# Moving the small tiles ahead of the large ones: a layout change in a hybrid gMLP and pooling layer

## The chip, the cores and the metric

The kernel runs on one core of one Trainium2 chip. The metric is the device time of one execution in microseconds; times given for a kernel are the median of several executions. One execution was also taken by the hardware profiler, and everything said about single instructions, waits and transfers comes from that one.

## The reference

One layer works on 4096 prompt frames and on 32 sample frames, with 1024 channels each. Cut to what matters here:

```python
h = rmsnorm(x, norm_g)
proj = jnp.einsum('btd,de->bte', h, w_in)                 # 1024 -> 5120
u, v, z_a, xb, z_b = jnp.split(proj, [...], axis=-1)      # five of 1024
v_n = layernorm(v, ln_v_g, ln_v_b)
a = u * chunk_mlp(v_n, w_spatial, b_spatial) * jax.nn.silu(z_a)   # 128x128 mixing of positions per head
b = pool_mix(x_ext, pos0, w_pool, pool_scale) * jax.nn.silu(z_b)  # windows 2/4/8/16, 256x256 map per group
y = x + jnp.einsum('bte,ed->btd', jnp.concatenate([a, b], axis=-1), w_out)   # 2048 -> 1024
return y, x_ext[:, -POOL_STATE:], v_n                     # y goes through a last rmsnorm
```

All inputs and outputs are float32. The outputs are the normalised y of prompt and sample, the last 15 pooling rows of both, and the v rows of the sample.

## The kernel before

**Products.** Each large product is cut into 2 x 2 blocks and made from seven block products in place of eight (the additions of the blocks before and after are on VectorE and ScalarE). Each operand is split into a high and a low part in the type float32r, and a block product is the sum of high x high, high x low and low x high. So a block product of one kind is 12 matmuls: four steps of 128 channels (k), three matmuls each. In the shared helper these are lines 175, 176 and 177; in the output product they are lines 698, 699 and 700. The moving operand is 512 columns wide, except in the last block of tokens, where 16 sample frames are added to each half and a product runs over two groups of 264 columns.

**Stages.** First the projection v is made for all tokens (0 to about 404 us of the span; moving operand: the weights of v, stationary operand: the split tokens). Then four blocks of 1024 tokens each go through eight gate sets (u and z of branch A, with the spatial mixing at line 913) and eight pool sets (the pooling map folded into the input weights, and z of branch B); here the moving operand is the tokens and the stationary one the split weights. The last two stages are the two halves of the output product (from about 1736 us on); the moving operand is the weights, the stationary one the split results.

**Tiles.** The moving operands lie in seven slots of 16896 bytes in each partition (pool slots, tile slot), one per block product, reloaded at each change of stage. In a block of tokens that is not the last, a slot holds for each part h and each channel step k four pieces of 128 columns, which stand 2048 bytes apart; one matmul reads all four. In the output stages and for v it reads 512 columns in one piece. In the last block of tokens the piece of part h and step k starts (4h + k) x 2112 bytes into the slot, and the second group of 264 columns 1056 bytes further. Loaded weights and results come into tiles raw (4096 bytes), are split into tiles wop (4096 bytes: high parts of four steps, then low parts), and sums go to tiles sum (2048 bytes). The v stage has tiles xt, op, h and et of the same kind in the same space. Results are gathered in tiles t (2176 bytes) and y (4096 bytes). Small tiles of 16 to 96 bytes (pool smallp) hold sums of squares, means and inverse roots; each name has its own ring of two.

**Where a tile lies.** Pools are laid one behind the other in each partition, in the order in which they are opened, and each tile is rounded up to a multiple of 32 bytes. Ahead of everything stand 16512 bytes that the kernel does not name; then the pool const (512 + 32 + 32 + 32 + 512 bytes), then the slots, then smallp, then the pools of the stages. So the slots start at byte 17632, and behind the 118272 bytes of slots and the 896 of smallp the stage pools start at 136800. The v tiles are laid from the other end and do not follow this order.

**Order.** The order of instructions on each engine is that of the code, with the preparation of operands (additions and splits) running five block products ahead of the matmuls that use them and the loads seven ahead. Loads go through the queue of SyncE, stores of results through that of GpSimd.

The lines that the change touches, besides the two pools: psc (the pooling scales), the small tile of OutPair.finish at line 718, and the two small tiles of OutSample at lines 754 and 775.

Of the kernel before, what the change touches and what calls it, by code (L numbers as in the profile page):

```python
# [8 lines left out]
F32 = mybir.dt.float32  # L9
# [6 lines left out]
P = 128  # L16
D = 1024
KT = D // P
SEQ = 4096
DEC = 32  # L20
# [16 lines left out]
def stream_step(ctx: ExitStack, tc, x_prompt, x_sample, state_pool, norm_g, w_in, ln_v_g, ln_v_b,  # L37
# [14 lines left out]
    w_out_v = w_out[0].rearrange("(k p) e -> k p e", p=P)  # L52

    const = ctx.enter_context(tc.tile_pool(name="const", bufs=1))
    slots = ctx.enter_context(tc.tile_pool(name="slots", bufs=NQ))
    smallp = ctx.enter_context(tc.tile_pool(name="smallp", bufs=2))
    dram = ctx.enter_context(tc.tile_pool(name="dram", bufs=1, space=bass.MemoryType.DRAM))

    abT = dram.tile([16, P, TOT], F32, name="abT")
# [11 lines left out]
    make_identity(nc, ident)  # L71
    lvg = const.tile([P, HEADS], F32, name="lvg")
    lvb = const.tile([P, HEADS], F32, name="lvb")
    psc = const.tile([P, KT], F32, name="psc")
    ppast = const.tile([P, KT, HALO], F32, name="ppast")

    def small(tag, n, rows=P):
        return smallp.tile([P, 8], F32, tag=tag, name=tag)[:rows, :n]
# [4 lines left out]
    def rsqrt(a, n, rows=P):  # L83

        y, t = small("rs_y", n, rows), small("rs_t", n, rows)
        nc.vector.tensor_single_scalar(t.bitcast(I32), a.bitcast(I32), 1, ALU.logical_shift_right)
        nc.vector.tensor_scalar(y.bitcast(I32), t.bitcast(I32), -1.0, float(0x5F3759DF), ALU.mult, ALU.add)
        for _ in range(3):
            nc.vector.tensor_tensor(t, y, y, ALU.mult)
            nc.vector.scalar_tensor_tensor(t, t, -0.5, a, ALU.mult, ALU.mult)  # L90
            nc.vector.scalar_tensor_tensor(y, t, 1.5, y, ALU.add, ALU.mult)
        return y
# [547 lines left out]
    class OutPair:  # L640
# [50 lines left out]
        def multiply(self, q):  # L691
            own = {0: 0, 1: 1, 2: 0, 3: 3, 4: 0, 5: 5, 6: 3}[q]
            if own == q:
                self.acc[own] = acc_tile()
            x, w = self.ops[q], w_slots[self.z, q]
            a, fresh = self.acc[own], own == q
            for k in range(4):
                mm(a, x[:, 0, k, :], w[:, k, 0], start=fresh and k == 0, stop=False, skip_group_check=True)  # L698
                mm(a, x[:, 0, k, :], w[:, k, 1], start=False, stop=False, skip_group_check=True)  # L699
                mm(a, x[:, 1, k, :], w[:, k, 0], start=False, stop=k == 3, skip_group_check=True)  # L700
            for n, h, bank in {0: [(0, 0, 0)], 1: [(0, 0, 1)], 2: [(1, 0, 0)], 3: [(1, 1, 3)], 4: [(0, 1, 0), (1, 1, 0)],
                               5: [(0, 1, 5)], 6: [(1, 0, 3)]}[q]:
                y = self.y[n][:, h * 512:(h + 1) * 512]
                nc.vector.tensor_tensor(y, self.acc[bank], y, ALU.add)  # L704
            if self.z and q in (1, 4, 5, 6):
                n, h = {1: (0, 0), 4: (1, 1), 5: (0, 1), 6: (1, 0)}[q]
                junk = sum_p.tile([P, 2 * 512], BF16, tag="sum", name="junk")[:, :512]
                nc.scalar.activation(junk, self.y[n][:, h * 512:(h + 1) * 512], AF.Square,
                                     accum_out=self.ss[:, n, h:h + 1])

        def finish(self, last=None):
            t0 = 2 * self.i * P
            if self.z == 0:
                for n in range(2):
                    nc.gpsimd.dma_start(part[t0 + n * P:t0 + (n + 1) * P, :], self.y[n])
                return
            tiles = (0, 1) if last is None else (last,)
            a = small("ssa", 2)
            ss, a = self.ss[:, tiles[0]:tiles[-1] + 1], a[:, :len(tiles)]
            nc.vector.tensor_tensor(a, ss[:, :, 0], ss[:, :, 1], ALU.add)  # L720
            nc.vector.tensor_scalar(a, a, 1.0 / D, EPS, ALU.mult, ALU.add)
            r = rsqrt(a, len(tiles))
            for n in tiles:
                y = self.y[n]
                for z, c in enumerate((slice(0, 512), slice(512, D)) if last is not None else (slice(0, D),)):
                    nc.vector.scalar_tensor_tensor(y[:, c], y[:, c], r[:, n - tiles[0]:n - tiles[0] + 1], f_bc[:, c],
                                                   ALU.mult, ALU.mult)
                    queue = nc.gpsimd if last is None else (nc.sync, nc.scalar)[z]
                    queue.dma_start(yp[t0 + n * P:t0 + (n + 1) * P, c], y[:, c])

    class OutSample:
# [19 lines left out]
        def multiply(self):  # L751
            b, w = self.both, w_slots
            if self.z:
                ss = small("sss", 2, DEC)
            for n, terms in enumerate(([(k, 0, k) for k in range(4)] + [(4 + k, 1, k) for k in range(4)],
                                       [(8 + k, 5, k) for k in range(4)] + [(12 + k, 3, k) for k in range(4)])):
                acc = more_tile()
                for i, (st, q, k) in enumerate(terms):
                    wq = w[self.z, q]
                    if i < 7:  # L760
                        mm(acc[:2 * DEC], b[:, st, :], wq[:, k, 0], start=i == 0, stop=False)  # L761
                    mm(acc[:DEC], b[:, st, :DEC], wq[:, k, 1], start=False, stop=False)  # L762
                mm(acc[:2 * DEC], b[:, st, :], wq[:, k, 0], start=False, stop=True)
                low = sum_p.tile([P, 512], F32, tag="sum", name="low")[:DEC]
                y = self.y[:, n * 512:(n + 1) * 512]
                nc.scalar.copy(low, acc[DEC:2 * DEC])
                nc.vector.tensor_tensor(y, low, y, ALU.add)
                nc.vector.tensor_tensor(y, acc[:DEC], y, ALU.add)
                if self.z:
                    junk = sum_p.tile([P, 2 * 512], BF16, tag="sum", name="junk")[:DEC, :512]  # L770
                    nc.scalar.activation(junk, y, AF.Square, accum_out=ss[:, n:n + 1])
            if self.z == 0:
                nc.gpsimd.dma_start(part[SEQ:], self.y)
                return
            a = small("ssb", 1, DEC)
            nc.vector.tensor_tensor(a, ss[:, :1], ss[:, 1:], ALU.add)
            nc.vector.tensor_scalar(a, a, 1.0 / D, EPS, ALU.mult, ALU.add)
            r = rsqrt(a, 1, DEC)
            nc.vector.scalar_tensor_tensor(self.y, self.y, r, f_bc[:DEC], ALU.mult, ALU.mult)
            nc.gpsimd.dma_start(ys, self.y)  # L780
# [303 lines left out]
    with ExitStack() as ph:  # L1084
# [7 lines left out]
        def more_tile():  # L1092
            return ps_more.tile([P, 512], F32, tag="more", name="more")
# [110 lines left out]
```

## Time and profile before

| | |
|---|---|
| median of 3 runs | 2397.96 us (2397.54 to 2403.63) |
| the profiled execution | 2398.71 us, span 2396.9 us |
| mean granted TensorE clock | 0.998 |
| TensorE matmul busy | 2375.3 us (99% of the span), 11924 instructions |
| weight loads busy | 1986.0 us (83%) |
| VectorE busy | 1795.2 us (75%) |
| ScalarE busy | 893.3 us (37%) |
| GpSimd busy | 201.3 us (8%) |
| moved by DMA | 445.69 MB, mean 186 GB/s |

How to read it: matmuls are pipelined, so the duration that a row shows for one matmul (about 0.4 us) is longer than the time from its start to the start of the next one. The pace of TensorE is read from starts and counts, not from durations; but where one matmul of a steady row takes longer than another, its duration grows too.

### The profile page before, as it was taken

To read this page: it belongs to the slowest core of one execution; us is meant where nothing else is said; L and a number is where in the kernel's file an instruction comes from. 1 tells how busy PE (TensorE), PEld (TensorE's weight loads), DVE (VectorE), ACT (ScalarE), POOL (GpSimd) and SP (SyncE) were. 2 spreads that over 40 slices of the span, in tenths; PEclk is the share of its full clock that TensorE was granted. 3 is DMA by queue.
4 is the path that set the end of the run, shared out by engine and by line. 5 is a ranking of instruction groups with operands and counts; after the bars stand their busy time and mean duration, and the time that the engine had idled before them with its cause. 6 is when DMAs were issued, how large, how long until landed. Compare 5 with 4: busy or idle time off the path is not lost.

```text
span 2396.9 us, 32564 instructions
## 1 busy us (share of the span) xinstructions
PE 2375.3 (99%) x11924; PEld 1986.0 (83%) x11924; DVE 1795.2 (75%) x3322; ACT 893.3 (37%) x1599; POOL 201.3 (8%) x394
## 2 busy tenths in 40 slices
PE   8999999999999999999999999999999999999998
PEld 6878887788888888888888899999977778888876
DVE  6877777766777667877668776668767777598887
ACT  6545444333433333333334333333322332233332
POOL 1010000100011000110001110102200000000000
PEclk9999999999999999999999999999999999999999
DMA  8878977432448334474334472334687777855432
GB/s 298 315 236 278 272 248 236 133 104 87 144 141 289 97 97 132 132 281 132 106 106 141 166 263 90 99 99 151 225 319 255 259 257 233 306 180 164 158 127 82
DMA packets 325289, 445.69 MB, mean 186 GB/s; under 512 B 19340, under 2 KB 248460, under 8 KB 322440
## 3 DMA queue, kind: packets, MB, share of 16 engines
q1 hardware_dynamic: 273384, 354.79, 45.2%
q0 software_dynamic: 22288, 73.48, 8.4%
q10 hardware_dynamic: 29456, 15.34, 2.4%
q8 instruction: 94, 1.54, 0.3%
q14 instruction: 67, 0.55, 0.1%
HBM read 273.88 MB, written 169.66 MB: 185 GB/s over the span
## 4 chain that ended last, share of the span: by engine, by line
PE 95%; DMA 3%; DVE 2%; ACT 0%; issue 0%; SPq 0%; DVEq 0%; ACTq 0%
PE acc L175 22%; PE acc L177 22%; PE acc L176 22%; PE acc L698 8%; PE acc L699 8%; PE acc L700 8%; PE sp L913 2%; PE tr L456 1%; DMA vt<-in_w_in_dram 1%; DMA wops<-raw 1%; DMA slot<-wops 1%; DMA op<-in_w_in_dram 0%; PE more L762 0%; DVE y L704 0%; PE more L761 0%
## 5 line engine op out<-in xcount | busy, mean ns | idle before, releaser
L175 PE MATMUL acc<-slot,wop 128*128 128x512 f32 (+1 forms) x2240 | 792.0, 354 | 2.1 <-ACT t L151 1.2
L177 PE MATMUL acc<-slot,wop 128*128 128x512 f32 (+1 forms) x2240 | 784.7, 351 | 0.0
L176 PE MATMUL acc<-slot,wop 128*128 128x512 f32 (+1 forms) x2240 | 784.5, 350 | 0.0
L175 PEld LDWEIGHTS acc<-slot,wop 128*128 128x128 f32 x2240 | 422.2, 188 | 61.2 <-ACT t L151 1.7
L177 PEld LDWEIGHTS acc<-slot,wop 128*128 128x128 f32 x2240 | 421.4, 188 | 60.1 <-DVE wop L81 0.3
L176 PEld LDWEIGHTS acc<-slot,wop 128*128 128x128 f32 x2240 | 422.1, 188 | 57.9 <-issue 0.2
L81 DVE TENSOR_TENSOR wop<-raw,wop 128x512 fp32r<-128x512 f32 x510 | 353.0, 695 | 154.7 <-ACT wop L106 137.7
L106 ACT CAST wop<-raw 128x512 fp32r<-128x512 f32 x340 | 210.5, 621 | 401.5 <-PE acc L177 321.0
L698 PE MATMUL acc<-slot,wop 128*128 128x512 f32 x896 | 353.8, 395 | 1.8 <-DMA slot<-wops 1.1
L699 PE MATMUL acc<-slot,wop 128*128 128x512 f32 x896 | 353.6, 395 | 0.0
L700 PE MATMUL acc<-slot,wop 128*128 128x512 f32 x896 | 353.2, 395 | 0.0
L149 DVE TENSOR_TENSOR t<-acc,t 128x512 f32<-128x512 f32 (+1 forms) x320 | 186.6, 584 | 129.8 <-ACT t L158 72.4
L704 DVE TENSOR_TENSOR y<-acc,y 128x512 f32<-128x512 f32 x256 | 173.4, 687 | 96.1 <-PE acc L700 94.7
L698 PEld LDWEIGHTS acc<-slot,wop 128*128 128x128 f32 x896 | 168.7, 188 | 43.8 <-ACT wop L660 2.4
L700 PEld LDWEIGHTS acc<-slot,wop 128*128 128x128 f32 x896 | 168.7, 188 | 39.6
L699 PEld LDWEIGHTS acc<-slot,wop 128*128 128x128 f32 x896 | 168.7, 188 | 39.2
L175 PE MATMUL acc<-slot,op 128*128 128x512 f32 x448 | 182.0, 407 | 0.3 <-ACT vt L151 0.2
L176 PE MATMUL acc<-slot,op 128*128 128x512 f32 x448 | 176.8, 395 | 0.0
L177 PE MATMUL acc<-slot,op 128*128 128x512 f32 x448 | 176.7, 396 | 0.0
L660 ACT CAST wop<-raw 128x512 fp32r<-128x512 f32 x160 | 97.9, 620 | 185.1 <-PE acc L700 172.3
L81 DVE TENSOR_TENSOR wop<-sum,wop 128x512 fp32r<-128x512 f32 x200 | 137.0, 685 | 30.0 <-ACT wop L106 24.6
L932 POOL DMA_DIRECT2D abT<-t x128 | 69.2, 541 | 874.6 <-DVE t L944 634.8
(213 smaller groups left out, 2489.3 us busy)
## 6 DMA issues: line engine op xcount, KB each, us to landing
raw<-in_w_in_dram SPq DMA_DIRECT2D x102, 512.0 KB, 4.3
xops<-op SPq DMA_DIRECT2D x72, 512.0 KB, 6.3
abT<-t POOLq DMA_DIRECT2D x128, 256.0 KB, 3.5
raw<-abT SPq DMA_DIRECT2D x64, 512.0 KB, 4.9
slot<-xops SPq DMA_DIRECT2D x30, 1024.0 KB, 10.6
slot<-wops SPq DMA_DIRECT2D x14, 2048.0 KB, 8.5
xt<-in_x_prompt_dram SPq DMA_DIRECT2D x32, 512.0 KB, 5.3
raw<-v_all SPq DMA_DIRECT2D x32, 512.0 KB, 3.4
```

The source lines that it names most:

```text
L81: return nc.vector.tensor_tensor(out, src, hi.bitcast(F32), ALU.subtract)
L106: pair = nc.scalar.copy(hi, src), lo_part(lo, src, hi)
L149: add = lambda o, x, y: nc.vector.tensor_tensor(o, x, y, ALU.add)
L175: mm(acc, sh, mh, start=fresh and k == 0, stop=False, skip_group_check=True)
L176: mm(acc, sh, ml, start=False, stop=False, skip_group_check=True)
L177: mm(acc, sl, mh, start=False, stop=k == 3, skip_group_check=True)
L660: nc.scalar.copy(t[:, 0], src)
L698: mm(a, x[:, 0, k, :], w[:, k, 0], start=fresh and k == 0, stop=False, skip_group_check=True)
L699: mm(a, x[:, 0, k, :], w[:, k, 1], start=False, stop=False, skip_group_check=True)
L700: mm(a, x[:, 1, k, :], w[:, k, 0], start=False, stop=k == 3, skip_group_check=True)
L704: nc.vector.tensor_tensor(y, self.acc[bank], y, ALU.add)
L932: nc.gpsimd.dma_start(abT[row, :, t0:t0 + HALF], t[:, :HALF])
```

## The change

The pool of small tiles is opened ahead of the slots in place of behind them. The tile psc is made four times as large, of which the first quarter is used. Three small names are given up: the sum of squares of the output pairs (ssa) uses the ring of ss, and the two of the output sample (sss and ssb) use the ring of nb. Nothing else is edited.

```diff
     const = ctx.enter_context(tc.tile_pool(name="const", bufs=1))
+    smallp = ctx.enter_context(tc.tile_pool(name="smallp", bufs=2))
     slots = ctx.enter_context(tc.tile_pool(name="slots", bufs=NQ))
-    smallp = ctx.enter_context(tc.tile_pool(name="smallp", bufs=2))
...
-    psc = const.tile([P, KT], F32, name="psc")
+    psc = const.tile([P, 4 * KT], F32, name="psc")[:, :KT]
...
-            a = small("ssa", 2)
+            a = small("ss", 2)
...
-                ss = small("sss", 2, DEC)
+                ss = small("nb", 2, DEC)
...
-            a = small("ssb", 1, DEC)
+            a = small("nb", 1, DEC)
```

In the built programs every engine has the same instructions in the same order with the same waits; the addresses of tiles in a partition are what differs:

| tile | bytes | start before, beyond a multiple of 512 | start after |
|---|---|---|---|
| slot | 16896 | 224 (first at 17632) | 0 (first at 18432) |
| raw, wop, sum, op, h, xt, et, y, spare | 2048 or 4096 | 96 (first at 136800) | 0 (first at 136704) |
| t | 2176 | 96, 224, 352, 480 in turn | 0, 128, 256, 384 in turn |
| WT, bias (spatial weights) | 4096 | 160 | 64 |
| v tiles | 4096 | 480 | 480 |
| ident | 512 | 128 | 128 |

The slots are 33 x 512 bytes long, so all seven start alike; so do the tiles of 2048 and 4096 bytes.

## The prediction, as written before the result

> **What bounds the kernel now.** I read the page first, for the engine that fills the span.
>
> ```profile
> span 2396.9 us, 32564 instructions
> PE 2375.3 (99%) x11924; PEld 1986.0 (83%) x11924; DVE 1795.2 (75%) x3322; ACT 893.3 (37%) x1599; POOL 201.3 (8%) x394
> PE 95%; DMA 3%; DVE 2%; ACT 0%; issue 0%; SPq 0%; DVEq 0%; ACTq 0%
> ```
>
> TensorE is busy for 99% of the span and is 95% of the chain that ended last. Next come the groups of its matmuls with the shapes kept apart.
>
> ```profile
> L175 PE MATMUL acc<-slot,wop 128*128 128x512 f32 x1344 | 534.6, 398 | 2.1 <-ACT t L151 1.2 <-ACT vt L295 0.8
> L176 PE MATMUL acc<-slot,wop 128*128 128x512 f32 x1344 | 530.4, 395 | 0.0
> L698 PE MATMUL acc<-slot,wop 128*128 128x512 f32 x896 | 353.8, 395 | 1.8 <-DMA slot<-wops 1.1 <-DVE y L704 0.7
> L699 PE MATMUL acc<-slot,wop 128*128 128x512 f32 x896 | 353.6, 395 | 0.0
> L176 PE MATMUL acc<-slot,wop 128*128 128x264 f32 x896 | 254.1, 284 | 0.0
> L176 PE MATMUL acc<-slot,op 128*128 128x512 f32 x448 | 176.8, 395 | 0.0
> ```
>
> The idle time ahead of them is a few microseconds in all, so hardly any wait can be shortened. Each count stands for three lines, so there are 3 x (1344 + 896 + 448) = 8064 wide matmuls (512 columns) and 3 x 896 = 2688 narrow ones (264). Their pace comes from the windows view, in two stretches that hold one shape alone.
>
> ```profile
> 630.00:740.00 110.00, 110.00 (x475) 1.00 0.56 185
> 1620.00:1730.00 110.00, 110.00 (x904) 1.00 0.51 174
> ```
>
> The engine is busy without a break at full granted clock. Counting those that began just before the window, a wide matmul follows the last one after (110 + 0.395) / 475 = 232.4 ns, a narrow one after (110 + 0.285) / 904 = 122.0 ns. So 8064 x 232.4 ns = 1874 us and 2688 x 122.0 ns = 328 us: 92% of the span is those two steps. **The change moves the time by what it does to these two numbers, and by little else.**
>
> **The change, part by part.** No instruction is added, removed or moved; each engine's order and waits are the same, only addresses change. Four edits go together:
>
> *Merged rings and the wider psc:* priced at 0. No wait appears in the program, and the small tiles are worked by VectorE, which is idle for a quarter of the span. Had one ring held a finish up, it would stand ahead of the additions at line 704 on VectorE, which free the accumulators.
>
> *VectorE and ScalarE at new addresses:* priced at 0. Line 149 works on t tiles, which already start at four places (96 to 480 beyond a multiple of 512), and on v tiles, which all start at 480:
>
> ```profile
> L149 DVE TENSOR_TENSOR t<-acc,t x320: 412/682/694, 423.6 to 1737.3; 128x512 f32<-128x512 f32 x96, 128x264 f32<-128x264 f32 x64
> L149 DVE TENSOR_TENSOR vt<-acc,vt x64: 680/691/694, 64.6 to 403.9; 128x512 f32<-128x512 f32 x64
> ```
>
> The longest is 694 ns in both, so a start place costs nothing that shows. If I am wrong, the slack of a quarter of the span covers some per cent.
>
> *Transfers:* the chain gives DMA 3%, about 72 us. Some of them touch tiles that move (op, slot, and raw as a source), some tiles that stay (vt):
>
> ```profile
> 3.19 6.69 DMA vt<-in_w_in_dram
> 13.19 9.60 DMA vt<-in_w_in_dram
> 32.86 7.96 DMA op<-in_w_in_dram
> 1733.99 12.26 DMA slot<-wops
> 1939.95 6.92 DMA wops<-raw
> ```
>
> No row has a transfer of one kind both ways. The load into op, beyond a multiple by 96, lies between two into vt, beyond it by 480. I take 0; the bound is the spread of the two loads into vt, 2.9 us either way.
>
> *Reads of TensorE:* the open cost. All wide matmuls now read a moving operand that starts 224 bytes beyond a multiple of 512 and a stationary one 96 beyond; afterwards both start on the multiple. Is the pace slow because of that? The upper bound on a gain is from the start of the kernel, where plain float32 matmuls of 256 columns run:
>
> ```profile
> 11.08 1.73 PE acc L244 x8
> ```
>
> 1.73 / 8 = 216 ns for 256 columns. If float32r takes half the time per column, 512 columns would take 216 ns and 264 about 112 ns. Against 232.4 and 122.0 that is 8064 x 16 + 2688 x 10 = 156 us above that floor. So there is something to win, if the start is what costs.
>
> The rows speak against most of it. First, line 176 reads four pieces of 128 columns and line 699 one piece of 512, from starts alike; if a start in the middle of some unit of memory cost an extra read, four pieces would pay it four times, yet both take 395 ns (rows above). Second, loading the weights, whose tiles start at 96, shows no loss either:
>
> ```profile
> L699 PEld LDWEIGHTS acc<-slot,wop x896: 187/188/192, 1736.7 to 2385.9; 128*128 128x128 f32 x180
> L699 PE MATMUL acc<-slot,wop x896: 390/393/404, 1737.0 to 2386.1; 128*128 128x512 f32 x180
> L762 PEld LDWEIGHTS more<-slot,wop x32: 107/108/112, 1777.3 to 2288.3; 128*32 128x32 f32 x32
> L762 PE MATMUL more<-slot,wop x32: 387/390/398, 1777.5 to 2288.5; 128*32 128x512 f32 x32
> ```
>
> From 32 to 128 columns it grows by 80 ns, 0.83 ns per column, with hardly a spread. Third, the narrow matmuls. In the last block of tokens a block product reads first the group that starts 32 bytes beyond a multiple of 64 (12 matmuls), then the group 1056 bytes further, which starts on a multiple of 64. The timeline of line 175 at the beginning of each group, three products in a row:
>
> ```profile
> 1640.14 0.29 PE L175 MATMUL acc<-slot,wop 128*128 128x264 f32 x1
> ...
> 1641.61 0.28 PE L175 MATMUL acc<-slot,wop 128*128 128x264 f32 x1
> ...
> 1643.07 0.29 PE L175 MATMUL acc<-slot,wop 128*128 128x264 f32 x1
> ...
> 1644.54 0.28 PE L175 MATMUL acc<-slot,wop 128*128 128x264 f32 x1
> ...
> 1645.99 0.29 PE L175 MATMUL acc<-slot,wop 128*128 128x264 f32 x1
> ...
> 1647.47 0.28 PE L175 MATMUL acc<-slot,wop 128*128 128x264 f32 x1
> ...
> 1648.92 0.29 PE L175 MATMUL acc<-slot,wop 128*128 128x264 f32 x1
> ```
>
> First groups: 1.47 + 1.47 + 1.48 = 4.42 us for 36 matmuls, 122.8 ns each. Second groups: 1.46 + 1.45 + 1.45 = 4.36 us, 121.1 ns. So a start on a multiple of 64 is worth about 1.7 ns, not 10. This is the nearest row there is for the moving operand; for the stationary one at another start there is none.
>
> **The sum.** Narrow matmuls: the groups change places (the first will start on the multiple, the second 32 beyond), so 0. Wide ones: all come to start on the multiple. If the 1.7 ns is per matmul, 8064 x 1.7 = 13.4 us; if per column, 512 / 264 times that, 26 us. I take 17 us, nearer the lower end, since part of the gain may be lost where other engines and transfers set the pace for a moment (the 12.26 and 6.92 us of DMA above). 2398.7 (the profiled execution) - 17 = 2381.7; its own time is 0.75 us above the median of the runs, so I say **2382 us**. Bounds of the open cost: a gain of 156 us, and a loss, from the longest form of line 699, of 8064 x (404 - 395) = 73 us.
>
> [...]
>
> **The rivals.**
>
> *Nothing changes: 2398 us.* The 232.4 ns would be the pace of this type of matmul from any start. For: four pieces and one cost the same, and the weight load costs 0.83 ns per column from a start at 96. Against: the 1.7 ns between the groups. [...]
>
> *The whole of it: 2398.7 - 156 = 2243 us.* Stationary operands away from a multiple would hold back the moving ones. For: no row has a float32r stationary operand on a multiple of 64. Against: with only 32 columns of weights (line 762) the median matmul is 390 ns against 393, so weights matter little.
>
> *Slower, by two reads that meet: 2435 us.* The weight load of the next matmul starts together with the running matmul:
>
> ```profile
> 1999.81 0.40 PE L698 MATMUL acc<-slot,wop 128*128 128x512 f32 x1
> 1999.81 0.19 PEld L699 LDWEIGHTS acc<-slot,wop 128*128 128x128 f32 x1
> ```
>
> Their starts are 128 bytes apart within 512 now and 0 apart afterwards. If the two reads then meet at the same place more often and one waits, more matmuls take the long form of 404 ns. The place is every wide matmul; if the mean goes half way from 395 to 404 ns, 8064 x 4.5 ns = 36 us more. It decides from 0.9 ns on (7 us). For: matmuls of one line already take 390 to 404 ns with no wait before them, so something about the timing costs. Against: line 762, as above.
>
> **How the numbers follow.** A measurement of this kernel tells about 0.3% (7 us) from no change. Moderate gain 0.40 (its own range 2362 to 2391), whole gain 0.10, no change 0.29, slower 0.21. Faster is 0.40 + 0.10 = 0.50, same 0.29, slower 0.21. The range, 2330 to 2420 us, leaves out the whole gain (0.10) and that part of the slower case above 2420 (about 0.09).
>
> **What would show it.** Right: line 699 has a median below 393 ns and fewer forms near 404; in a window of wide matmuls alone the step falls from 232.4 to about 230 ns; in the last block of tokens the first group becomes the quicker of the two; weight loads stay at 188 ns, line 149 at 694 ns at most. The first rival: the same 475 matmuls in 110 us. The whole gain: about 510. The slower one: below 468, with the 404 ns form common. Wrong altogether would be a shift that sits in waits, in transfers or on VectorE while the step stays at 232.4 ns.

## The result and the profile after

The changed kernel takes 2353.89 us (median; 2352.39 to 2357.39) beside 2400.3 us for the kernel before on the same chip (2397.54 to 2403.63; four runs, the three given above among them). The ratio is 0.9815, with a 95% interval of 0.9803 to 0.9826: **1.85% faster**, some 46 us where 17 were forecast. The profiled execution took 2352.39 us.

The page of the changed kernel, the same rows as before the change: span, engines, chain of waits.

```profile
span 2350.6 us, 32564 instructions
PE 2330.3 (99%) x11924; PEld 1980.8 (84%) x11924; DVE 1790.2 (76%) x3322; ACT 893.8 (38%) x1599; POOL 211.5 (9%) x394
PE 90%; issue 4%; DMA 3%; DVE 2%; ACT 1%; POOL 0%; SPq 0%; DVEq 0%; POOLq 0%; ACTq 0%
```

The busy time of TensorE fell by 45.0 us (2375.3 to 2330.3) and the span by 46.3; VectorE stayed near 1790 us (1795.2 to 1790.2) and ScalarE at 894. So the time went from the matmuls themselves. The 4% of issue in the chain lie mostly between 1744 and 1830 us, where the chain goes back through the stores of line 715; TensorE is busy there without a break (90.00 of the 90 us from 1740 to 1830). The groups by shape (busy us and mean ns of one, then the idle time ahead of them):

```profile
L175 PE MATMUL acc<-slot,wop 128*128 128x512 f32 x1344 | 527.5, 393 | 2.1 <-ACT t L151 1.2 <-ACT vt L295 0.8
L176 PE MATMUL acc<-slot,wop 128*128 128x512 f32 x1344 | 523.4, 389 | 0.0
L698 PE MATMUL acc<-slot,wop 128*128 128x512 f32 x896 | 349.1, 390 | 3.1 <-DVE y L704 1.9 <-DMA slot<-wops 1.2
L699 PE MATMUL acc<-slot,wop 128*128 128x512 f32 x896 | 348.8, 389 | 0.0
L176 PE MATMUL acc<-slot,wop 128*128 128x264 f32 x896 | 254.1, 284 | 0.0
L176 PE MATMUL acc<-slot,op 128*128 128x512 f32 x448 | 175.2, 391 | 0.0
```

Line 176 was 395 ns and is 389, line 699 was 395 and is 389; the narrow form is 284 ns in both. The idle times ahead are a few microseconds still. The windows view gives the pace, wide matmuls in the first row, narrow ones in the second:

```profile
630.00:740.00 110.00, 110.00 (x487) 1.00 0.66 232
1600.00:1700.00 100.00, 100.00 (x826) 1.00 0.53 184
```

(110 + 0.389) / 487 = **226.7 ns** for a wide step, where it was 232.4; (100 + 0.284) / 826 = 121.4 ns for a narrow one, where it was 122.0. The clock granted is the full one in both (1.00). One line, with its weight loads:

```profile
L699 PEld LDWEIGHTS acc<-slot,wop x896: 187/188/190, 1704.3 to 2339.5; 128*128 128x128 f32 x180
L699 PE MATMUL acc<-slot,wop x896: 388/389/397, 1704.5 to 2339.7; 128*128 128x512 f32 x180
```

Not only the median fell (393 to 389 ns): the whole spread did, from 390 to 404 down to 388 to 397. A weight load takes 188 ns as before.

**Where the 46.3 us came from.** Adding up all distances from the start of one matmul to the start of the next in the two traces: all 8191 wide float32r matmuls (the 8064 and some of the sample frames) 1922.6 to 1880.7 us, so 42 us; narrow ones 330.5 to 329.3, so 1; all the others, plain float32 matmuls and transposes with the waits among them, 131.8 to 128.6, so 3. That is the whole difference. The last 3 us are hardly the work of the addresses: 2.9 of them lie in the group of line 244 in the first 50 us, where single steps of 1 to 2 us are waits, and a run below with both operands at 64 has the same step of the wide matmuls and 131.8 us there again. Leaving out the 135 or so steps of over 260 ns, behind which stands a wait or another kind of matmul, the mean wide step is 232.6 ns before and 227.2 after. This figure, formed alike for every run, is called the wide step below.

The steps also changed in kind. In the changed kernel they are 225 to 228 ns one after the other; before, they went through repeating patterns such as 232, 228, 230, 233, 241, 232, 231. That looks less like a slower stream than like one that is held up again and again.

### The profile page after: what moved, and what is told of

Same layout as the page of the kernel before. It is cut to its first block, busy times and chain, and to the rows that moved or that the text cites. A ratio compares the mean times of both kernels' runs of the same rounds, so it can differ in the third digit from the quotient of the medians.

```text
span 2350.6 us, 32564 instructions
## 1 busy us (share of the span) xinstructions
PE 2330.3 (99%) x11924; PEld 1980.8 (84%) x11924; DVE 1790.2 (76%) x3322; ACT 893.8 (38%) x1599; POOL 211.5 (9%) x394
## 4 chain that ended last, share of the span: by engine, by line
PE 90%; issue 4%; DMA 3%; DVE 2%; ACT 1%; POOL 0%; SPq 0%; DVEq 0%; POOLq 0%; ACTq 0%
PE acc L175 22%; PE acc L177 22%; PE acc L176 22%; PE acc L698 6%; PE acc L699 6%; PE acc L700 6%; PE sp L913 2%; DMA wops<-raw 1%; PE tr L456 1%; DMA vt<-in_w_in_dram 1%; DMA slot<-wops 1%; DVE y L704 1%; PE acc L244 0%; DMA op<-in_w_in_dram 0%; DVE wop L81 0%
## 5 line engine op out<-in xcount | busy, mean ns | idle before, releaser
L698 PE MATMUL acc<-slot,wop 128*128 128x512 f32 x896 | 349.1, 390 | 3.1 <-DVE y L704 1.9
L699 PE MATMUL acc<-slot,wop 128*128 128x512 f32 x896 | 348.8, 389 | 0.0
L700 PE MATMUL acc<-slot,wop 128*128 128x512 f32 x896 | 348.4, 389 | 0.0
```

## The experiments

Each run below differs from the changed kernel (or from the one before, where said) by the lines shown. "Moving at" and "stationary at" are the starts of the slots and of the tiles wop and op, in bytes beyond a multiple of 512: 224 and 96 before the change, 0 and 0 after. The distance is stationary minus moving, within 256 bytes.

### The rings alone

The kernel before, with the three small names merged as in the change; an unused gap of 192 bytes takes the place of what they leave, so that the large tiles lie where they lay.

```diff
     smallp = ctx.enter_context(tc.tile_pool(name="smallp", bufs=2))
+    padp = ctx.enter_context(tc.tile_pool(name="padp", bufs=1))
+    padp.tile([P, 48], F32, name="gap")
...
-            a = small("ssa", 2)
+            a = small("ss", 2)
...
-                ss = small("sss", 2, DEC)
+                ss = small("nb", 2, DEC)
...
-            a = small("ssb", 1, DEC)
+            a = small("nb", 1, DEC)
```

> The merged rings alone; pools in the old order, the space of the three small names filled up, so that every large tile lies where it lay before. If addresses are all that counts: the step of before (232.4 ns) and 2398 us. If the rings are worth anything: below that with the same step.

Measured: 2397.6 us (one run) beside 2399.23, wide step 232.7 ns. The merged rings are worth nothing that can be told. What remains is addresses.

### One operand at a time

Only the moving operand on the multiple (the stationary one back at 96):

```diff
     slots = ctx.enter_context(tc.tile_pool(name="slots", bufs=NQ))
+    padp = ctx.enter_context(tc.tile_pool(name="padp", bufs=1))
+    padp.tile([P, 24], F32, name="gap")
```

> The changed kernel with an unused gap of 96 bytes behind the slots: the slots (moving operands) stay on multiples of 512, all stage tiles (raw, op, wop, sum; the stationary operands) go back to 96 beyond one. If the moving start alone sets the step: 226.7 ns per wide matmul as in the changed kernel, about 2354 us. If the stationary start alone: 232.4 ns, about 2398 us. If the distance between the two starts counts (128 before, 0 after, 416 here): anything but 226.7 ns. If merged rings, VectorE or transfers made the gain: 2354 us with a step that explains nothing.

Only the stationary operand on the multiple (the moving one back at 224):

```diff
-    smallp = ctx.enter_context(tc.tile_pool(name="smallp", bufs=2))
     slots = ctx.enter_context(tc.tile_pool(name="slots", bufs=NQ))
+    smallp = ctx.enter_context(tc.tile_pool(name="smallp", bufs=2))
+    padp = ctx.enter_context(tc.tile_pool(name="padp", bufs=1))
+    padp.tile([P, 24], F32, name="gap")
...
-    psc = const.tile([P, 4 * KT], F32, name="psc")[:, :KT]
+    psc = const.tile([P, KT], F32, name="psc")
```

> The merged rings, but the pool of small tiles behind the slots and filled up so that the slots start 224 beyond a multiple of 512 as before and the stage tiles on a multiple. Moving start alone: 232.4 ns and about 2398 us. Stationary start alone: 226.7 ns and about 2354 us. Both needed: 232 ns. Distance: not 226.7 ns.

Measured: 2412.16 us, ratio 1.0056 [1.0041, 1.0071], and 2402.82 us, ratio 1.0014 [1.0004, 1.0024]: both slower than the kernel before. The windows of wide matmuls, moving operand on the multiple first, then stationary:

```profile
630.00:740.00 110.00, 110.00 (x472) 1.00 0.54 180
```

```profile
630.00:740.00 110.00, 110.00 (x473) 1.00 0.54 182
```

The wide steps are 234.2 and 233.3 ns. Neither start alone brings a part of the gain, so two gains that add up are ruled out. Either both must be on a multiple, or something between the two counts.

### Both away from the multiple

All large tiles moved together, by 64 bytes and by 32 (5 in place of 6):

```diff
-    psc = const.tile([P, 4 * KT], F32, name="psc")[:, :KT]
+    psc = const.tile([P, 6 * KT], F32, name="psc")[:, :KT]
```

> The changed kernel with psc 64 bytes longer, so that slots and stage tiles all start 64 beyond a multiple of 512. If a multiple of 64 is enough (the rows of the narrow groups): 226.7 ns, 2354 us. If 128 or more is needed: slower than 228 ns, above 2362 us. If only the distance of the two starts counts (0 here as in the changed kernel): 226.7 ns.

> The changed kernel with psc 32 bytes longer: slots and stage tiles all 32 beyond a multiple of 512, distance 0 where before had 128. If only the place within 64 bytes counts, this is the case of before (224 and 96 are both 32 beyond a multiple of 64): 232.4 ns, 2398 us. If the distance alone counts: 226.7 ns, 2354 us.

Measured: 2356.73 and 2354.95 us; wide step 227.1 and 227.2 ns. The window of the run with both at 32:

```profile
630.00:740.00 110.00, 110.00 (x487) 1.00 0.64 219
```

487 matmuls, as in the changed kernel, though neither the slots nor the tiles wop and op start on a multiple of 64 any more. **So it is not alignment. What counts is that both start alike.**

### Groups of 256 and 272 columns in the last block

If the start of the narrow groups mattered (the row that the prediction's 1.7 ns came from), a second group that also starts on a multiple of 64 should have gained:

```diff
-                self.groups = [(0, HALF)] if not self.last else [(0, WIDE // 2), (WIDE // 2, WIDE // 2)]
+                self.groups = [(0, HALF)] if not self.last else [(0, HALF // 2), (HALF // 2, WIDE - HALF // 2)]
```

> The changed kernel; in the last block of tokens the 528 columns are cut into 256 and 272 in place of 264 and 264, so that the second group starts 1024 bytes further, on a multiple of 64 like the first. [...]

Measured: 2356.45 us, ratio 0.9821 [0.9804, 0.9839], not to be told from the changed kernel. The narrow steps are 118.0 ns for 256 columns and 125.7 for 272, 121.9 in the mean where two groups of 264 have 121.4. At the pace per column of the wide ones (226.7 / 512 ns) they would be 113.4 and 120.4 ns, an estimate. Nothing gained.

### A map of the distance

The moving operand stays at 0, the stationary one goes to 32, 64, 160, 192, 224 and 256 by the size of the gap (8, 16, 40, 48, 56 and 64 elements):

```diff
+    padp = ctx.enter_context(tc.tile_pool(name="padp", bufs=1))
+    padp.tile([P, 48], F32, name="gap")
```

> The changed kernel with a gap of 32 bytes behind the slots: slots on a multiple, stage tiles 32 beyond. If only the place within 64 bytes counts, it equals the run with the stage tiles at 96: 234.2 ns, 2412 us. If the distance counts: another step.

> The changed kernel with an unused gap of 64 bytes behind the slots: slots on a multiple of 512, stage tiles 64 beyond one; both on multiples of 64, but 64 bytes apart within 512. If only the places within 64 bytes count: 226.7 ns, 2354 us, as for both at 0 and both at 64. If the distance of the two starts counts too: 230 ns or more, above 2375 us.

> Stage tiles 160 beyond a multiple of 512, slots on one. Any distance but 0 alike: 232 to 235 ns, 2397 to 2415 us. Dependent on which read is ahead: another step than at 96 (234.2 ns).

> Stage tiles 192 beyond a multiple of 512, slots on one. If any distance but 0 costs about alike: 232 to 235 ns, 2397 to 2415 us. If the cost depends on which of the two reads is ahead: another step than at 64 (233.3 ns), perhaps below 226.7 ns.

> Stage tiles 224 beyond a multiple of 512, slots on one. Any distance but 0 alike: 232 to 235 ns, 2397 to 2415 us. Dependent on which read is ahead: another step than at 32 (233.2 ns), perhaps below 226.7 ns.

> The changed kernel with a gap of 256 bytes behind the slots: slots on a multiple of 512, stage tiles 256 beyond one. If the distance of the two starts repeats every 256 bytes (the narrow matmuls of the runs with distances 288 and 32 have the same pattern): 226.7 ns, 2354 us. If every 512: above 230 ns, 2395 us or more.

All in one table, with the runs above:

| moving at | stationary at | distance within 256 | wide step, ns | time, us |
|---|---|---|---|---|
| 0 | 0 | 0 | 227.2 | 2353.89 |
| 64 | 64 | 0 | 227.1 | 2356.73 |
| 32 | 32 | 0 | 227.2 | 2354.95 |
| 0 | 256 | 0 | 227.2 | 2355.26 |
| 0 | 32 | 32 | 233.2 | 2406.00 |
| 224 | 0 | 32 | 233.3 | 2402.82 |
| 0 | 64 | 64 | 233.3 | 2402.88 |
| 0 | 96 | 96 | 234.2 | 2412.16 |
| 224 | 96 (before) | 128 | 232.6 | 2400.30 |
| 0 | 160 | 160 | 233.3 | 2404.74 |
| 0 | 192 | 192 | 229.2 | 2373.41 |
| 0 | 224 | 224 | 233.3 | 2403.28 |

The time is the median of four runs or more in the rows 0 and 0, 0 and 96, 224 and 0, and before; in the others it is one run, and the step, a mean over some 8050 matmuls, is the firmer figure.

The windows at 256 and at 192 bytes:

```profile
630.00:740.00 110.00, 110.00 (x487) 1.00 0.66 228
```

```profile
630.00:740.00 110.00, 110.00 (x482) 1.00 0.63 217
```

One distance in eight is fast, 192 stands between, six are slow, and a shift of 256 changes nothing (227.2 ns at 0 and at 256). The two ways to a distance of 32 agree within 0.1 ns. At 192 the steps repeat in threes (226, 229, 232 ns), and which of the three lines has which changes along the trace. The kernel before stood on one of the slow distances by its order of pools.

### Which stationary operand?

A matmul runs while the weights of the next one are loaded: at 644.84 us of the changed kernel a matmul of line 175 starts (0.39 us) and with it the load for the matmul of line 176 (0.19 us) that starts at 645.07. To tell a matmul's own weights from the next one's, the low parts alone were moved by 96 bytes in the token and output stages. They are the weights of lines 177 and 700 of the changed kernel, and are loaded while lines 176 and 699 run. To make room, wop has six buffers.

```diff
-    op_p = pool("wop_p", 7)
+    op_p = pool("wop_p", 6)
...
-    def weight_tile():
-        return op_p.tile([P, 2, 4, P], F32R, tag="wop", name="wop")
+    def weight_tile(shifted=False):
+        t = op_p.tile([P, 1152], F32R, tag="wop", name="wop")
+        if shifted:
+            return t[:, :512].rearrange("p (k t) -> p k t", k=4), t[:, 536:1048].rearrange("p (k t) -> p k t", k=4)
+        return t[:, :1024].rearrange("p (h k t) -> p h k t", h=2, k=4)
...
-                self.ops[q] = t = weight_tile()
+                self.ops[q] = t = weight_tile(True)
...
```

> The changed kernel with one piece of the stationary tile moved: in the token and output stages the low parts of the split weights (or results) start 96 bytes further, the high parts stay at distance 0 from the moving operand; the ring of tiles wop has six buffers in place of seven. Only one of the three matmuls of a step has the low part as its stationary operand (lines 177 and 700), and its weights are loaded while the one before it runs (lines 176 and 699). If a running matmul is slowed by the load of the next weights (theory A): the step of the matmuls of lines 176 and 699 goes from 226.7 to about 233.5 ns, the median of line 699 from 389 to about 394 ns, and lines 175, 177, 698 and 700 stay. If it is slowed by the place of its own weights (theory B): the same, but on lines 177 and 700. Either way 2240 wide matmuls by some 6.5 ns are about 15 us more: about 2369 us. If all three lines change alike, the cost lies in the stream as a whole and neither theory holds; if nothing changes, the distance of the low parts doesn't matter.

Measured: 2392.97 us beside 2398.75; both theories named there fell. The groups of the token stages, by shape:

```profile
L175 PE MATMUL acc<-slot,wop 128*128 128x512 f32 x1344 | 536.1, 400 | 5.6 <-DVE t L149 3.5 <-ACT t L151 1.2 <-ACT vt L295 0.8
L177 PE MATMUL acc<-slot,wop 128*128 128x512 f32 x1344 | 529.4, 395 | 0.0
L176 PE MATMUL acc<-slot,wop 128*128 128x512 f32 x1344 | 529.2, 394 | 0.0
```

All three lines lost their gain, not one: from 393, 389 and 389 ns to 400, 394 and 395. Their wide steps are 233.1, 231.7 and 232.6 ns. Nearly the whole gain is gone although two of three weight tiles are where they should be. Two more runs asked whether cutting the tile did it, and how far one wrong distance reaches. First, against that run, 256 bytes in place of 96:

```diff
-            return t[:, :512].rearrange("p (k t) -> p k t", k=4), t[:, 536:1048].rearrange("p (k t) -> p k t", k=4)
+            return t[:, :512].rearrange("p (k t) -> p k t", k=4), t[:, 576:1088].rearrange("p (k t) -> p k t", k=4)
```

> As the run with the low parts 96 bytes further, but 256 bytes further: the same split tile and the same number of buffers, only the distance to the moving operand is again a multiple of 256. If the distance of the low parts was what slowed all three lines there, the step goes back to 226.7 to 227.2 ns and the time to about 2357 us (2353 to 2361). If cutting the tile in two, or the gap in it, was the cause, the time stays near 2393 us.

Measured: 2359.41 us, wide step 227.3 ns:

```profile
L175 PE MATMUL acc<-slot,wop 128*128 128x512 f32 x1344 | 528.4, 394 | 5.7 <-DVE t L149 3.1 <-ACT t L151 1.2 <-ACT vt L295 0.8
L176 PE MATMUL acc<-slot,wop 128*128 128x512 f32 x1344 | 523.3, 389 | 0.0
L177 PE MATMUL acc<-slot,wop 128*128 128x512 f32 x1344 | 522.5, 389 | 0.0
```

The cut costs nothing; the 96 bytes do. These two runs differ in nothing but the place of the low parts, so the other tiles that moved along in the table above (raw, sum, t, y) are not needed to explain the loss. Second, the 96 bytes only in the first of each seven block products, again shown against the run with 96:

```diff
-    def weight_tile(shifted=False):
+    def weight_tile(split=False, shifted=False):
         t = op_p.tile([P, 1152], F32R, tag="wop", name="wop")
-        if shifted:
-            return t[:, :512].rearrange("p (k t) -> p k t", k=4), t[:, 536:1048].rearrange("p (k t) -> p k t", k=4)
+        s = 536 if shifted else 512
+        if split:
+            return t[:, :512].rearrange("p (k t) -> p k t", k=4), t[:, s:s + 512].rearrange("p (k t) -> p k t", k=4)
...
-                self.ops[q] = t = weight_tile(True)
+                self.ops[q] = t = weight_tile(True, q == 0)
...
-                    t = weight_tile(True)
+                    t = weight_tile(True, q == 0)
```

> The low parts are 96 bytes further only in the first of seven block products of each set or output pair; all other stationary operands keep distance 0. If a wrong distance slows its own matmul and the few around it (theory C: short memory), only that product has steps near 232.5 ns, the others 226.7: the mean of the wide matmuls there is about 226.9 + 5.6 / 7 = 227.7 ns, the time 5 us above the run without the shift, about 2362 us. If a wrong distance throws the stream out of step for long (theory D: the cheap step is a state that needs an undisturbed run of equal distances to be found again), the products after it stay near 232.5 ns as well and the time goes towards 2393 us; in the order of products this shows as steps that fall only some way into the undisturbed run.

Measured: 2363.29 us, 4 us above the run before it. The mean step of each matmul from the start of a disturbed product of twelve (80 such products of wide matmuls in the trace, steps of over 260 ns left out; the low parts are the 3rd, 6th, 9th and 12th; from 13 on the next product, which is not disturbed). In the run before it the same 24 places have 226.6 to 227.2 ns.

| matmul | 1 | 2 | 3 | 4 | 5 to 11 | 12 | 13 | 14 | 15 | 16 | 17 | 18 to 24 |
|---|---|---|---|---|---|---|---|---|---|---|---|---|
| step, ns | 227.5 | 228.5 | 230.3 | 234.6 | 228.5 to 233.9 | 230.5 | 234.5 | 228.2 | 231.4 | 230.2 | 226.8 | 226.6 to 226.8 |

The short memory (theory C) holds: behind the last weights at a wrong distance four matmuls are still held up, from the fifth on the step is 226.6 to 226.8 ns again. So one wrong distance in three matmuls reaches all of them, which is what the run with all low parts at 96 bytes showed. For the same reason these runs can't say whether a matmul's own weights or the next one's are the partner; that the step rises already at the matmul ahead of the first wrong weights (228.5 ns, where the run before it has 227.2) speaks for the load that runs beside it, but is no proof.

The two runs whose only difference is the address of the low weights take 2392.97 and 2359.41 us: how fast the matmuls follow each other depends on where the weights lie.

### Narrow matmuls at distance 0

In the last block the moving pieces stand 2112 bytes apart and the stationary ones 512, so their distance changes from step to step. The control has the six buffers and the groups of 256 and 272 columns:

```diff
-    op_p = pool("wop_p", 7)
+    op_p = pool("wop_p", 6)
...
+        t = op_p.tile([P, 1152], F32R, tag="wop", name="wop")
+        return t[:, :1024].rearrange("p (h k t) -> p h k t", h=2, k=4)
```

> The control for the next run: the changed kernel with six wop buffers of 4608 bytes in place of seven of 4096, and groups of 256 and 272 columns in the last block of tokens. The sixth buffer less should cost nothing that can be told (the preparation runs five products ahead): 2356 us (2353 to 2360), as the run with the groups alone. Wide steps stay at 226.7 to 227.2 ns, narrow ones at 121.9 ns in the mean.

The run sets the stationary pieces 576 bytes apart there, so that every narrow matmul and its own weights are at distance 0:

```diff
+        if last:
+            return t.rearrange("p (h k t) -> p h k t", h=2, k=4)[:, :, :, :P]
```

> As the control, but in the last block of tokens the pieces of the stationary tile stand 576 bytes apart in place of 512, as the moving pieces stand 2112 apart: both pitches are 64 beyond a multiple of 256, so a matmul and its own weights start at distance 0. [...] If narrow matmuls are bound by something else (the load of 128 columns takes 188 ns, longer than their step of 122): no change, within 2 us of the control.

Measured: control 2359.12 us, ratio 0.9833 [0.9818, 0.9847]; with the pieces at distance 0 2361.29 us, ratio 0.9839 [0.9823, 0.9855]: no gain. Line 176, control first:

```profile
L176 PE MATMUL acc<-slot,wop 128*128 128x272 f32 x448 | 128.3, 286 | 0.0
...
L176 PE MATMUL acc<-slot,wop 128*128 128x256 f32 x448 | 126.0, 281 | 0.0
```

```profile
L176 PE MATMUL acc<-slot,wop 128*128 128x272 f32 x448 | 128.9, 288 | 0.0
...
L176 PE MATMUL acc<-slot,wop 128*128 128x256 f32 x448 | 125.7, 281 | 0.0
```

The steps are 118.0 and 125.7 ns in the control, 118.4 and 126.0 here. The distance to their own weights doesn't move narrow matmuls. What holds them stays open, and two causes fit: the next weights are still 64 bytes off for every third matmul, and if those are the partner, one in three is enough to reach all (as with the low parts above); or something else binds. The weight load, at 188 ns longer than their step, is the obvious rival, and loads are under way for 99.6% of this stage (342.59 of the 344 us from 1360 to 1704 in the changed kernel). But the loads overlap there (three in a row start at 1640.45, 1640.57 and 1640.70 us and take 0.19 us each), and the step follows the columns of the matmul, 118.0 ns for 256 and 125.7 for 272 (a ratio of 1.065, that of the columns is 1.0625), though each has the same 128 columns of weights to load. That speaks against a fixed cost of each load, and no run settles it. The sixth buffer less cost more than nothing (2359.12 us against 2356.45 with seven), so the two are compared with each other only.

### Transposes in the v stage

In the changed kernel the wide step of the v stage is 228.9 ns, where the token stages have 226.9. Transposes (line 456) stand between those matmuls, and their two operands are 128 bytes apart. Moving ident by 128 bytes makes it 0:

```diff
+    lvg = const.tile([P, HEADS], F32, name="lvg")
+    lvb = const.tile([P, HEADS], F32, name="lvb")
+    psc = const.tile([P, 2 * KT], F32, name="psc")[:, :KT]
     ident = const.tile([P, P], F32, name="ident")
     make_identity(nc, ident)
-    lvg = const.tile([P, HEADS], F32, name="lvg")
-    lvb = const.tile([P, HEADS], F32, name="lvb")
-    psc = const.tile([P, 4 * KT], F32, name="psc")[:, :KT]
+    const.tile([P, 2 * KT], F32, name="pad")
```

> The changed kernel with the tile ident 128 bytes further in its pool, so that the transposes of line 456 (457 here) also read their two operands at distance 0 within 256 bytes, where they now have 128. In the v stage of the changed kernel the wide matmuls next to a transpose take 228 to 236 ns and those away from one 226 to 227 (mean 228.9). If a wrong distance disturbs its neighbours over a few matmuls, those next to the transposes fall too: at most 1375 x (228.9 - 226.9) = 2.8 us, so 2351 us (2350.5 to 2353), and a mean of the wide matmuls of the v stage near 227.5 ns. If they are slow for another reason (the change of the kind of matmul, the wait for the transposed tile), the mean stays at 228.9 ns and the time at 2353.9 us.

Measured: 2354.56 us, ratio 0.9815 [0.9802, 0.9828], the same as the change alone; the wide step of the v stage 228.6 ns. Nearly all of the excess stays, so the distance of the transposes is not its cause. No run was faster than the changed kernel.

## Why the prediction was right or wrong

**What bounds the kernel: right.** The change moved the time by the two steps and by little else: 43 of 46 us are the wide and narrow ones. The other 3 lie at the start of the kernel, in waits that differ by as much between runs with the same step.

**Parts priced at 0: right.** The merged rings alone gave 2397.6 us. On VectorE the lines at new addresses are as they were; line 149 after:

```profile
L149 DVE TENSOR_TENSOR t<-acc,t x320: 414/682/694, 415.2 to 1705.7; 128x512 f32<-128x512 f32 x96, 128x264 f32<-128x264 f32 x64
L149 DVE TENSOR_TENSOR vt<-acc,vt x64: 679/691/693, 61.5 to 395.9; 128x512 f32<-128x512 f32 x64
```

The share of DMA in the chain is 3% as before.

**Narrow matmuls at 0: right in size.** 1.2 us in all. The groups did change places as forecast: by the medians of their twelve matmuls the first went from 122.8 to 120.9 ns, the second from 121.1 to 122.1. But they do not tell what they were read to tell: with both groups on a multiple of 64, nothing was gained.

**The step that failed: "Wide ones: all come to start on the multiple ... I take 17 us".** The term was built on 1.7 ns per matmul from the two narrow groups, the nearest row there was; it measured 5.4 ns (232.6 to 227.2), 42 us over all wide matmuls of the two traces, and with it most of the 46. Not only the size was off, the mechanism was: starting on a multiple is worth nothing. Tiles at 32 and 64 bytes beyond it run as fast as at 0 provided both operands are there, and one operand on the multiple alone is slower than before. The row was taken from matmuls whose distances change from step to step and which gained, in the mean, half a nanosecond at most from any layout tried, so neither a factor per column (26 us) nor one per matmul (13 us) could have been right. That the forecast had the direction right is luck: the change brought both operands to a multiple of 512 and, with that, to distance 0, and only the second counts. The time lies inside the range given, but below the 2362 us at which the moderate gain was to end.

**The weights were dismissed by a wrong row.** Line 762, with only 32 columns of weights and a median of 390 against 393 ns, was read as "weights matter little". The durations hide what the starts show. The matmuls of lines 761 to 763 stand in two runs of 32 by themselves, all with 32 or 64 columns of weights. In the kernel before, their steps are 229.8 ns in the mean where the stream has 232.6, and nine in a row take 224 to 228 ns, the pace that the rest reached only by the change. In the changed kernel, at distance 0, their mean is 230.3 ns beside a stream of 227. So the columns of weights did bear on the pace, and the rule of the distance is shown for loads of 128 columns alone; what sets the pace of the shorter ones stays open.

**The slower rival had the mechanism, with the wrong sign.** "Two reads that meet": it took the starts of the moving operand and the next weights, 128 bytes apart within 512 before and 0 after, and held that reads which start alike collide. The distance is indeed what decides (whether with the next weights or the own ones is open), and 0 is the one place in eight at which the stream is disturbed least. No row of the kernel before told the sign, since the wide matmuls of its large products all stood at one distance.

**No change (2398 us)** took the equal cost of four pieces and one as a sign that no start counts. They still cost the same (389 ns each), and both became faster. All distances tried are multiples of 32 bytes, and the step still differs by 7 ns.

**The whole of it (2243 us)** did not come either: 226.7 ns is still 11 ns above the 216 ns taken from line 244, at no distance tried is the mean wide step below that of distance 0, and the narrow ones hardly moved. Of the 16.4 ns between 232.4 and 216 the distance explains 5.7. Line 244 has its 216 ns for 256 columns of plain float32; that float32r takes half the time per column was the author's assumption, and no run shows it: 0.84 ns there (216 / 256), 0.44 for the wide ones at distance 0 (226.7 / 512).

**What would show it:** the median of line 699 below 393 ns, weight loads at 188, line 149 at 694 at most, the swap of the groups: all four came. The step "to about 230 ns" came as 226.7, which by the prediction's own signs (475 none, about 510 the whole) was a third of the way, 487.

## What to carry to other kernels

Where TensorE is busy all the time with equal matmuls and the step between their starts is uneven, look at the start addresses of moving and stationary tiles: here it paid to have them equal within 256 bytes, 2% of the whole kernel, at no cost but the order of pools and a padded tile, and putting only one of the two on a round address lost time. This is shown for matmuls of 512 columns with loads of 128 columns of weights; narrower ones did not follow it. It has to hold for all stationary tiles of the stream, because one in three at another distance took nearly the whole gain. A difference between rows of another shape is a poor price for such a change; a few runs with one pool shifted by steps of 32 bytes would have told more than all rows of the trace.

## What the runs showed of the hardware

- The pace of 512-column float32r matmuls with 128-column weight loads beside them depends on the distance between the two operands' starts: 226.7 ns in steady stretches at 0, 229.2 in the mean at 192, 232.6 to 234.2 at the other distances in steps of 32. A shift of 256 bytes made no difference: 227.2 ns in the mean at 0 and at 256, 233.2 and 233.3 at 32 and 288. At 0, 32, 96, 128 and 192 bytes the median weight load of the output product's second line is 188 ns each time, that of its matmul 389, 396, 397, 393 and 388.
- Behind the last weights at a wrong distance the disturbance lasts for four matmuls, 0.9 us (234.5 + 228.2 + 231.4 + 230.2 ns), then the stream is back at 226.6 to 226.8 ns.
- Narrow matmuls take 122.0 ns in the mean in the kernel before, 121.4 in the changed one, 121.9 in groups of 256 and 272 and 122.2 with their own weights at distance 0. That is 0.46 ns per column (118.0 / 256, 121.4 / 264, 125.7 / 272), where the wide ones at distance 0 take 0.44 (226.7 / 512).
- Wide matmuls with weights of 32 and 64 columns take 229.8 ns in the mean at distance 128 and 230.3 at distance 0: the gain was not theirs.
- Why the distance counts, and with which of the two weight tiles, stays open: the records show when a matmul and a load start, not which read waits.
